# Rotating the start address of weight pairs inside their slots, in the feed-forward stage of a hybrid decoder block

## The chip, the cores and the metric

The kernel runs on one core of one Trainium2 chip. The time is device time in microseconds, from the runs of the whole program; the runs of before are given by their median. A profile is one more execution, recorded instruction by instruction. The engines are called by the profile's names: PE (TensorE's matmuls), PEld (TensorE's weight loads), DVE (VectorE), ACT (ScalarE), POOL (GpSimd) and SP (SyncE, which issues most DMAs).

## The reference

One decoder block on 1024 tokens of width 1024, in float32. Two branches (a diagonal state-space model and a forgetting attention) are merged by gates; then come cross-attention into 256 memory tokens, a SwiGLU feed-forward with 2816 hidden channels, and a last norm:

```python
h = h + (gate_a * out_a + gate_b * out_b) @ w_mix_out[l]
h = h + memory_cross_attention(rms_norm(h, norm_mem_q[l]), rms_norm(mem, norm_mem_kv[l]),
                               w_mem_q[l], w_mem_kv[l], w_mem_o[l])
f_a, f_b = jnp.split(rms_norm(h, norm_ffn[l]) @ w_ffn_in[l], 2, axis=-1)
h = h + (jax.nn.silu(f_a) * f_b) @ w_ffn_out[l]
...
return rms_norm(h, norm_final)
```

The change lies in the feed-forward, in the product with `w_ffn_in` (the first product) and at the beginning of the product with `w_ffn_out` (the second).

## The kernel before, in words

All products are computed from float32 values that are split in two: a high part in the type float32r, which ACT casts, and a low part, the rest, which DVE subtracts (`split`, lines 178 and 179). A product of two split values is three matmuls: high by high, high by low, low by high. Each has 128 rows, 128 columns of weights and up to 512 columns of moving operand, and comes with a weight load of its own.

The first product runs over 22 blocks of 128 hidden channels (`j`). In each block the 2x2 arrangement of token halves and of the two weight halves is computed by seven products instead of eight (Strassen's way, in Winograd's form). The token operands A11, A12, A22 and S1 to S4 are made once and stay in SBUF; the weight operands are made per block:

- `w_first(j)` splits the block's first weights, 128x1024, into one pair of tiles. Its two halves are the weights of products 1 and 2, which `start(j)` runs with A11 and A12.
- `w_sums(j)` makes sums of the weights and splits them into a second pair, in two steps of 128x512 (products 5 and 6, with S1 and S2), and into one more tile `we` (product 7, with S3). `middle(j)` runs these.
- `w_last(j)` fills `wdh` and `wdl` for products 3 and 4 (S4 and A22), which `end(j)` runs.

Each of the seven products is `prod` (line 868): four steps of 128 rows by three matmuls, 12 matmuls. A block is thus 84 matmuls.

The pairs of `w_first` and `w_sums` come from `wpair`: two tiles with the tags `whi` and `wlo`, each from a ring of four slots. A ring hands its slots out in turn, and a slot is filled anew when the last matmul that reads it is done. A slot holds `WSLOT` = 1088 values of 4 bytes in each partition, 4352 bytes, of which a pair uses the first 1024 values. `we`, `wdh`, `wdl` and the first pair of block 0 (`wh0`, `wl0`) come from other slots of 4096 bytes. The same two rings serve the stages ahead of the feed-forward, through other helpers.

For blocks 0 and 1 (`AHEAD_IN` = 2) the weight operands were made earlier, during the mixing product, and kept in DRAM (`w_d`). `w_kept` fetches them from there by DMA, 512 KB per tile, in the place of the split.

In the second product `o_get` splits operands of 128x1024 of which one half is the weights and the other the moving operand. Its first four pairs (`m < 4`) come from `wpair` too, the later ones from other slots. Each pair serves 12 matmuls (line 1005).

In the attention stage earlier on, the tiles `vhi` and `vlo` hold the split values: in a row of `vhi` each of 2 x 8 heads has 65 columns of 4 bytes, in `vlo` 64. They are written in lines 1457 and 1458 and used as weights in lines 1645, 1646 and 1652.

A scheduler sets the order of instructions on each engine when the kernel is built; it goes by the dependences between tiles and by its own due times.

Of the kernel before, what the change touches and what calls it, by code (L numbers as in the profile page):

```python
# [10 lines left out]
F32R = mybir.dt.float32r  # L11
# [8 lines left out]
P = 128  # L20
D = 1024
# [12 lines left out]
WSLOT = 1088  # L34
# [258 lines left out]
def hybrid_block_kernel(ctx: ExitStack, tc: tile.TileContext, x, mem, norm_mix, w_in, b_forget,  # L293
# [35 lines left out]
    with tc.tile_pool(name="st2", bufs=1, reuse_waits="tile") as s2:  # L329
        stage_tail(B, big, s2, sh, x, glu, aT, gate_d, kv_d, w_fox_o, w_mix_out, norm_mem_q[0], w_mem_q,  # L330
                   w_mem_o, norm_ffn[0], w_ffn_in, w_ffn_out, norm_final, out)
# [166 lines left out]
def stage_tail(B, big, s2, sh, x, glu, aT, gate_d, kv_d, w_fox_o, w_mix_out, g_mq, w_mem_q, w_mem_o, g_ffn,  # L498
# [7 lines left out]
    def slot(dt=F32, name="t"):  # L506
        return s2.tile([P, D], dt, tag="t", bufs=NS2, name=name)
# [289 lines left out]
        put("S4", bslot, i, y[:, :512])  # L797
        put("A22", bslot, i, y[:, 512:])

    raws, wts, ev = {}, {}, {}  # L800

    def w_fetch(j):
        raws[j] = B.wpool.tile([P, RAW], F32, tag="raw", bufs=4, name="raw")[:, :D], tmp("rawb")
# [5 lines left out]
    def wpair(j):  # L809
        if j < 0:  # L810
            return slot(F32R, "wh0"), slot(F32R, "wl0")
        return [B.wpool.tile([P, WSLOT], F32R, tag=t_, name=t_)[:, :D] for t_ in ("whi", "wlo")]

    def w_kept(j, n, t_):
        S.dma_start(f32(t_), w_d[j, n])
# [1 line left out]
    def w_first(j):  # L817

        if j < AHEAD_IN:
            a_ = wpair(j - 1 if j == 0 else j)  # L820
            for i, t_ in enumerate(a_):
                w_kept(j, i, t_)
            wts[j, 1], wts[j, 2] = [[t_[:, o:o + 512] for t_ in a_] for o in (0, 512)]
            return
        ra, rb = raws[j]
        a_ = wpair(j - 1 if j == 0 else j)
        B.split(*a_, ra)
        wts[j, 1], wts[j, 2] = [[t_[:, o:o + 512] for t_ in a_] for o in (0, 512)]

    def w_sums(j):  # L830
        b_, e_ = wpair(j), slot(F32R, "we")
        if j < AHEAD_IN:
            for i, t_ in enumerate((*b_, e_)):
                w_kept(j, 2 + i, t_)
            wts[j, 5], wts[j, 6] = [[t_[:, o:o + 512] for t_ in b_] for o in (0, 512)]
            wts[j, 7] = e_[:, :512], e_[:, 512:]
            return
        ra, rb = raws[j]
        b22 = rb[:, 512:]
        V.tensor_add(ra[:, 512:], ra[:, 512:], b22)  # L840
        V.tensor_add(ra[:, :512], ra[:, :512], rb[:, :512])
        V.tensor_add(rb[:, :512], rb[:, :512], b22)
        wts[j, 5], wts[j, 6] = [[t_[:, o:o + 512] for t_ in b_] for o in (0, 512)]
        wts[j, 7] = e_[:, :512], e_[:, 512:]
        B.split(*wts[j, 5], ra[:, :512])
        V.tensor_add(ra[:, 512:], ra[:, 512:], ra[:, :512])
        V.tensor_add(ra[:, :512], ra[:, :512], b22)
        B.split(*wts[j, 6], ra[:, :512])
        B.split(*wts[j, 7], rb[:, :512])
# [961 lines left out]
```

## Time and profile before

| | |
|---|---|
| runs | 1594.38, 1594.53, 1589.32 us |
| median | 1594.38 us |
| span of the profiled execution (the only time the profile has of it) | 1592.0 us |
| mean granted clock of TensorE | 0.984 |
| busy: PE, PEld, DVE, ACT, POOL | 1538.3, 1265.5, 1023.0, 655.8, 257.4 us |
| first product's matmuls | from about 942 to 1373 us of the span |

In the profile a row of a group reads: line, engine, operation, tiles written and read (buffer numbers left out), shapes, count. A row of an order of time begins with its start and its length in microseconds; a bracket at its end tells how long the engine was idle before it and what ended that. PE's matmuls overlap, so the time from one start to the next is what a matmul costs in a stream, and it is called the step below. A row of what touches a tile gives the least, the median and the greatest length in nanoseconds.

### The profile page before, as it was taken

How to read it: one execution, taken by the hardware profiler on the slowest of the kernel's cores; microseconds unless marked ns; L12 is line 12 of the kernel's file. 1: busy time of each engine (PE TensorE's matmuls, PEld its weight loads, DVE VectorE, ACT ScalarE, POOL GpSimd, SP SyncE). 2: the span in 40 equal slices, each digit the busy share in tenths (PEclk: the TensorE clock that was granted, in tenths of full speed). 3: DMA queues.
4: the chain of work that ended last, by engine and by line, in shares of the span. 5: the costliest groups of instructions: out<-in, count | busy, mean ns of one | idle time of the engine just before them, and what ended most of it. 6: DMA issues, size and time to landing. Idle time of an engine off the chain costs nothing.

```text
span 1592.0 us, 20434 instructions
## 1 busy us (share of the span) xinstructions
PE 1538.3 (97%) x7313; PEld 1265.5 (79%) x7313; DVE 1023.0 (64%) x1822; ACT 655.8 (41%) x1173; POOL 257.4 (16%) x339
## 2 busy tenths in 40 slices
PE   7799989999999899999999989999999999999997
PEld 6688878898777578878888778888888888788885
DVE  6756535444688777776455687777777775565555
ACT  6423334322566553232335564333333333354342
POOL 3037453200121114210001200010000000000001
PEclk8999999999999999999999999999999999999999
DMA  8763556332022746457403176555544443896542
GB/s 293 150 110 96 134 107 125 84 144 29 13 57 46 198 110 200 132 178 257 154 22 98 53 272 237 160 166 167 164 159 158 159 149 129 277 392 223 191 153 106
DMA packets 197941, 240.86 MB, mean 151 GB/s; under 512 B 35448, under 2 KB 126488, under 8 KB 197328
## 3 DMA queue, kind: packets, MB, share of 16 engines
q1 hardware_dynamic: 191216, 223.84, 47.7%
q10 hardware_dynamic: 6624, 15.73, 2.6%
q8 instruction: 57, 0.93, 0.2%
q14 instruction: 44, 0.36, 0.1%
HBM read 165.60 MB, written 75.86 MB: 152 GB/s over the span
## 4 chain that ended last, share of the span: by engine, by line
PE 79%; DVE 7%; DMA 6%; ACT 3%; POOL 2%; issue 2%; SPq 1%; DVEq 0%; POOLq 0%; ACTq 0%
PE mm L868 15%; PE mm L168 8%; PE mm L169 8%; PE mm L170 8%; PE pv L868 7%; PE mm L1005 4%; PE sc L868 4%; PE sc L168 3%; PE sc L170 3%; PE sc L169 3%; PE sc L1005 3%; PE pv L1005 3%; PE misc L1005 1%; DMA raw<-in_w_in_dram 1%; DMA raw<-in_w_mem_kv_dram 1%
## 5 line engine op out<-in xcount | busy, mean ns | idle before, releaser
L178 ACT CAST whi<-raw 128x1024 fp32r<-128x1024 f32 (+2 forms) x124 | 116.0, 941 | 178.0 <-PE mm L868 48.6
L179 DVE TENSOR_TENSOR wlo<-raw,whi 128x1024 fp32r<-128x1024 f32 (+2 forms) x121 | 130.9, 1086 | 75.2 <-ACT whi L178 73.1
L168 PE MATMUL mm<-uh,whi 128*128 128x512 f32 x344 | 138.5, 403 | 2.2 <-ACT whi L178 2.2
L170 PE MATMUL mm<-uh,wlo 128*128 128x512 f32 x344 | 135.9, 396 | 0.5 <-DVE wlo L179 0.5
L169 PE MATMUL mm<-ul,whi 128*128 128x512 f32 x344 | 136.4, 397 | 0.0
L179 DVE TENSOR_TENSOR ol<-or,oh 128x1024 fp32r<-128x1024 f32 x73 | 89.3, 1224 | 70.8 <-ACT oh L178 69.6
L178 ACT CAST oh<-or 128x1024 fp32r<-128x1024 f32 x73 | 76.8, 1053 | 103.3 <-PE mm L1005 35.2
L900 POOL TENSOR_TENSOR g<-a,c 128x512 f32<-128x512 f32 x22 | 35.3, 1603 | 392.8 <-ACT a L899 392.8
L197 POOL TENSOR_TENSOR r<-ms,mhalf 128x1 f32<-128x1 f32 (+1 forms) x30 | 17.9, 597 | 373.0 <-DVE ms L193 345.6
L168 PEld LDWEIGHTS mm<-uh,whi 128*128 128x128 f32 x344 | 66.0, 192 | 14.9 <-ACT whi L178 2.7
L170 PEld LDWEIGHTS mm<-uh,wlo 128*128 128x128 f32 x344 | 65.5, 190 | 14.9 <-DVE wlo L179 1.5
L1630 POOL TENSOR_TENSOR pl<-pf,ph 128x512 fp32r<-128x512 f32 (+1 forms) x32 | 37.8, 1181 | 244.5 <-DVE ph L1629 174.6
L169 PEld LDWEIGHTS mm<-ul,whi 128*128 128x128 f32 x344 | 65.8, 191 | 11.1
L1627 ACT ACTIVATE pf<-sc 128x512 f32<-128x512 f32 (+1 forms) x96 | 46.3, 489 | 44.9 <-DVE sc L1623 29.2
L868 PE MATMUL pv<-S3h,we 128*128 128x512 f32 x176 | 58.1, 389 | 0.0
L1633 DVE TENSOR_TENSOR pl<-pf,ph 128x512 fp32r<-128x512 f32 (+2 forms) x64 | 36.2, 567 | 10.1 <-ACT ph L1632 9.3
L1100 POOL TENSOR_TENSOR sg<-sg,ga 128x512 f32<-128x512 f32 x16 | 29.9, 1890 | 73.3 <-DVE sg L1093 73.0
L1005 PE MATMUL mm<-oh 128*128 128x512 f32 x106 | 41.2, 389 | 0.0
L1005 PE MATMUL mm<-ol,oh 128*128 128x512 f32 x106 | 41.2, 389 | 0.0
L1005 PE MATMUL mm<-oh,ol 128*128 128x512 f32 x106 | 41.2, 389 | 0.0
L168 PE MATMUL sc<-uh,whi 128*128 128x512 f32 x104 | 40.9, 393 | 0.0
L168 PE MATMUL mm<-yh,whi 128*128 128x512 f32 x104 | 40.7, 392 | 0.0
(579 smaller groups left out, 4558.3 us busy)
## 6 DMA issues: line engine op xcount, KB each, us to landing
or<-c_d SPq DMA_DIRECT2D x77, 256.0 KB
raw<-in_w_in_dram SPq DMA_DIRECT2D x22, 512.0 KB
wo<-in_w_ffn_out_dram SPq DMA_DIRECT2D x22, 512.0 KB
c_d<-g SPq DMA_DIRECT2D x44, 256.0 KB
t_d<-wo SPq DMA_DIRECT2D x44, 256.0 KB
or<-t_d SPq DMA_DIRECT2D x44, 256.0 KB
raw<-in_w_ffn_in_dram SPq DMA_DIRECT2D x20, 512.0 KB
rawb<-in_w_ffn_in_dram SPq DMA_DIRECT2D x20, 512.0 KB
```

The lines of the kernel that those rows point to most:

```text
L168: T.matmul(ps, lh, rh, start=first, stop=False)
L169: T.matmul(ps, lh, rl, start=False, stop=False)
L170: T.matmul(ps, ll, rh, start=False, stop=last)
L178: self.A.copy(hi, src)
L179: (self.G if pool_lo else self.V).tensor_sub(lo, src, f32(hi))
L868: T.matmul(ps, l_[:, k, :], r_, start=first and k == 0 and i == 0, stop=k == 3 and i == 2, skip_group_check=True)
L900: G.tensor_mul(g[:, 512:], a1, c1)
L1005: T.matmul(ps, l_[:, gi], r_[:, 512:], start=n < 3 and p == 0 and k == 0 or n == 7 and p == 0 and k == 0, stop=p == NP - 1 and k == 2, ski ...
L1100: self.B.G.tensor_mul(self.out[j][:, cs], self.out[j][:, cs], ga)
L1627: self.exp = A.activation(pf[:, off:], ps[:, off:], AF.Exp)
L1630: G.tensor_sub(pl[:, off:], pf[:, off:], f32(ph[:, off:]))
L1633: V.tensor_sub(pl[:, off:], pf[:, off:], f32(ph[:, off:]))
```

## The change

`wpair` counts the pairs that it takes from the rings. Pair number n no longer begins at the first byte of its slots but 16·(n mod 16) bytes into them, from 0 to 240 bytes, in `whi` and in `wlo` alike. The slots, their size, their number and what is written into them stay; 1088 values leave room for 1024 values and an offset of up to 60. Pairs that don't come from the rings (`j < 0`) are not counted.

```diff
-    raws, wts, ev = {}, {}, {}
+    raws, wts, ev, npair = {}, {}, {}, [0]
...
     def wpair(j):
         if j < 0:
             return slot(F32R, "wh0"), slot(F32R, "wl0")
-        return [B.wpool.tile([P, WSLOT], F32R, tag=t_, name=t_)[:, :D] for t_ in ("whi", "wlo")]
+        o = 4 * (npair[0] % 16)
+        npair[0] += 1
+        return [B.wpool.tile([P, WSLOT], F32R, tag=t_, name=t_)[:, o:o + D] for t_ in ("whi", "wlo")]
```

The numbers run in the order of the calls: 0 is `w_sums(0)`, then `w_first(j)` has 2j − 1 and `w_sums(j)` has 2j, up to 42; the four pairs of the second product are 43 to 46.

## The prediction

> **What bounds the kernel now.** I read the page first, then the stretches of the feed-forward stage, then what TensorE waited for there, then single instructions. The page gives the engines, the granted clock and the chain that ended last:
>
> ```profile
> PE 1538.3 (97%) x7313; PEld 1265.5 (79%) x7313; DVE 1023.0 (64%) x1822; ACT 655.8 (41%) x1173; POOL 257.4 (16%) x339
> ...
> PE 79%; DVE 7%; DMA 6%; ACT 3%; POOL 2%; issue 2%; SPq 1%; DVEq 0%; POOLq 0%; ACTq 0%
> ```
>
> PE holds 97% of the span and 79% of the chain. The edited helper works from about 940 us on. Busy time by stretch (PE, weight loads, DVE, ACT, POOL, then granted clock and DMA):
>
> ```profile
> 930.00:960.00 30.00, 26.00 (x119) 21.36 (x118) 25.61 (x57) 16.06 (x42) 2.03 (x3) 0.89 0.89 316
> 1000.00:1100.00 100.00, 100.00 (x443) 82.81 (x442) 75.42 (x108) 37.23 (x60) 7.89 (x5) 1.00 0.55 175
> 1200.00:1300.00 100.00, 100.00 (x443) 82.81 (x442) 69.77 (x97) 36.16 (x59) 7.89 (x5) 1.00 0.48 152
> ```
>
> From 1000 us on TensorE is busy all the time at full clock, and nobody else is. What TensorE waited for between 930 and 1400 us, all of it:
>
> ```profile
> PE misc L223 <- DVE rt L202: 2.6, 1, 2.6
> PE mm L868 <- DMA whi<-w_d: 1.4, 1, 1.4
> PE mm L868 <- ACT c L889: 1.1, 1, 1.1
> PE sc L1005 <- DVE ol L179: 0.2, 1, 0.2
> ```
>
> So 5.3 us of waiting in 470 us, and none of it for the ACT or DVE half of a weight split. The stage lasts as long as its matmuls last. A piece of PE's order of time shows the step from one to the next:
>
> ```profile
> 1049.60 0.39 PE L868 MATMUL pv<-A22h,wdh 128*128 128x512 f32 x1
> 1049.83 0.39 PE L868 MATMUL pv<-A22l,wdh 128*128 128x512 f32 x1
> ...
> 1051.41 0.39 PE L868 MATMUL pv<-A22h,wdl 128*128 128x512 f32 x1
> 1051.64 0.39 PE L868 MATMUL mm<-S2h,whi 128*128 128x512 f32 x1
> 1051.87 0.39 PE L868 MATMUL mm<-S2l,whi 128*128 128x512 f32 x1
> ```
>
> From 1049.60 to 1051.64 are nine steps, 226.7 ns each. The 0.39 us is one matmul's passage; they overlap. The step is the same for weights in the general slots (wdh, wdl) and in the rotating ring (whi, wlo).
>
> **The change part by part.** It adds no instruction, takes none away and moves none: every engine has the same instructions in the same order with the same waits, and every tile keeps its place. What differs is a start address in 1132 instructions. Of the pairs that `wpair` hands out in rotation, number n starts 16·(n mod 16) bytes into its slot. There are 47: 43 for the first product and 4 for the beginning of the second. Pairs 0, 16 and 32 stay where they were. That leaves 40 × 24 + 4 × 12 = 1008 matmuls and their weight loads, 60 ACT casts, 60 DVE subtractions and 4 DMAs with another address. Before, every slot starts at remainder 192 of 256 bytes. Now the odd n, which are the pairs of `w_first` and two of the last four, start 16 bytes off a 32-byte boundary: 21 × 24 + 2 × 12 = 528 matmuls. The even ones stay on 32 bytes.
>
> Weight loads. The nearest rows are in the attention stage: head h of `vhi` starts 260·h bytes into its half, so its loads start at all of 0, 4, ... 28 past 32 bytes; `vlo` heads start at multiples of 256 bytes from their slot. From what touches these two tiles, min/median/max in ns:
>
> ```profile
> L1645 PEld LDWEIGHTS pv<-ph,vhi x96: 133/135/184, 403.6 to 608.4; 128*65 128x65 f32 x96
> L1646 PEld LDWEIGHTS pv<-ph,vlo x96: 133/134/231, 403.9 to 608.5; 128*64 128x64 f32 x96
> L868 PEld LDWEIGHTS mm<-S2h,whi x88: 187/188/188, 963.0 to 1358.1; 128*128 128x128 f32 x88
> ```
>
> Eight remainders against one, and the median differs by 1 ns with one column more. So I cost the changed loads at nothing: 1008 × 0 = 0. There is cover as well. Loads of the same 128x128 form, before shorter matmuls, started this often:
>
> ```profile
> 398.36 0.19 PEld L169 LDWEIGHTS sc<-wlo,uh 128*128 128x128 f32 x1
> 398.47 0.19 PEld L170 LDWEIGHTS sc<-whi,ul 128*128 128x128 f32 x1
> ...
> 400.87 0.19 PEld L169 LDWEIGHTS sc<-wlo,uh 128*128 128x128 f32 x1
> 400.99 0.19 PEld L170 LDWEIGHTS sc<-whi,ul 128*128 128x128 f32 x1
> ```
>
> Twenty-one steps from 398.47 to 400.99 are 120 ns each, so loads overlap one another and one needs at most 120 ns of its port. Under a step of 226.7 ns, 107 ns are spare. The two ends: a load whose step doubles to 240 ns shows 13.3 ns per matmul; one that gains as much as 64 columns cost twice over (188 less 134 is 54 ns, so 108) and overlaps nothing takes 296 ns, 69 ns more than the step: 528 × 69 = 36.6 us. Below nothing: see the second rival.
>
> Moving operand. The four pairs of the second product are read as moving operand too, two of them off 32 bytes: 24 matmuls. No row has a moving operand off 32 bytes; I take nothing, as with the loads, and as the upper end twice the step: 24 × 226.7 ns = 5.4 us.
>
> ACT and DVE. The nearest writes are again those of `vhi`: half of them start 16 past 32 bytes, half on it, and DVE's subtraction reads them back:
>
> ```profile
> L1457 ACT CAST vhi<-mm x9: 372/372/374, 328.6 to 396.6; 128x256 fp32r<-128x256 f32 x9
> L1458 DVE TENSOR_TENSOR vlo<-mm,vhi x9: 417/425/425, 329.0 to 397.0; 128x256 fp32r<-128x256 f32 x9
> ```
>
> 372 to 374 ns over both kinds: nothing again. Were a split twice as long, here is what covers it, one wide split in the middle of the stage:
>
> ```profile
> 1046.17 1.05 ACT L178 CAST whi<-raw 128x1024 fp32r<-128x1024 f32 x1 [0.55 <-PE sc L868]
> 1047.26 1.23 DVE L179 TENSOR_TENSOR wlo<-raw,whi 128x1024 fp32r<-128x1024 f32 x1 [0.17 <-ACT whi L178]
> ```
>
> ACT starts it as soon as PE has let go of the slot. A block is 84 matmuls, 19.0 us; two pairs of the four-slot ring are filled per block, so the pair is read more than a block later. Per block ACT casts 1.05 + 2 × 0.62 us into the ring and DVE subtracts 1.23 + 2 × 0.69, about 2.6 us; doubled, DVE goes from 70% to 84% and ACT from 36% to 48%. Neither becomes the bound.
>
> DMA. Pairs 1 and 2 are not split but fetched, 512 KB for each half. Pair 2 (32 bytes) is not waited for. Pair 1 (16 bytes) is:
>
> ```profile
> 946.56 0.45 SPq L815 DMA_DIRECT2D whi<-w_d  x1
> 947.05 0.44 SPq L815 DMA_DIRECT2D wlo<-w_d  x1
> ...
> 952.80 0.80 PE L868 MATMUL mm<-A11h,whi 128*128 128x512 f32 x1 [1.38 <-DMA whi<-w_d]
> 953.39 0.63 PE L868 MATMUL mm<-A11l,whi 128*128 128x512 f32 x1
> 953.82 0.63 PE L868 MATMUL sc<-A12h,whi 128*128 128x512 f32 x1
> ```
>
> Its price is that of the third rival; I take nothing, since rows of 4 KB start off a 256-byte boundary before and after.
>
> Sum: 0 on every term. The profiled execution has a span of 1592.0 us; the median of the runs is 1594.38, 2.4 us above. I forecast the median unchanged, **1594.4 us**.
>
> **The rivals.** First, slower: the weight load, one place. If a 16-byte-odd start doubles the load's step, the 528 odd matmuls cost 528 × 13.3 ns = 7.0 us (1601.4); if any start that differs from its neighbours' does it, 1008 × 13.3 = 13.4 us (1607.8); without overlap 36.6 us (1631). It decides from 15.1 ns per odd matmul, which is 8.0 us or 0.5%, about what a measurement of this kernel can tell from no change. For it: no row has a full 128-column load at such a start. Against it: the eight remainders of `vhi` and 107 ns to spare.
>
> Second, faster: all operands share remainder 192 of 256, and that costs something which spreading removes. At 953.39 to 953.82, in the half-clock stretch (0.89 on average there), the step is 430 ns, so 215 at full clock, while 226.7 is seen: some 12 to 13 ns per matmul are not columns. If address spreading removed 13.3 ns from 1008 matmuls, the time is 1594.4 − 13.4 = 1581. Against it: the `vhi` loads are already spread over many remainders, and the steps there are no shorter:
>
> ```profile
> 421.35 0.39 PE L1645 MATMUL pv<-ph,vhi 128*65 128x512 f32 x1
> 421.58 0.39 PE L1646 MATMUL pv<-ph,vlo 128*64 128x512 f32 x1
> 421.81 0.39 PE L1652 MATMUL pv<-pl,vhi 128*65 128x512 f32 x1
> 422.04 0.22 PE L1620 MATMUL sc<-hb 69*128 69x128 f32 x1
> ```
>
> 230 ns each. And the waits offer only 5.3 us, 0.3%, even if all went.
>
> Third, the fetch of pair 1 lands later. Two halves of 0.52 MB at the 316 GB/s of that stretch are 3.3 us; doubled, PE waits 3.3 us more, and the half-clock stretch that follows the idle (953.39 to about 958) may come once more, some 2.4 us lost. 1594.4 + 5.7 = 1600.1, still within 0.5%. The Trainium skill, Collectives: The Full Stack, section Rules for kernel authors, asks for buffers on 32 bytes because that prevents a read-modify-write; taken over to this fetch, pair 1 would pay it and pair 2 would not. It speaks of collectives' buffers, and no row here has a fetch at such a start.
>
> That the change does nothing of what it says is excluded: the addresses do differ.
>
> **How the numbers follow.** Forecast 0.83; slower load 0.09, of which 0.07 beyond 0.5%; faster steps 0.05; late fetch 0.03. Within 0.5%: 0.83 + 0.02 + 0.03 = 0.88. The shown runs lie from 1589.32 to 1594.53, so a median may fall 5 us to either side with nothing changed, 1589 to 1600. The range takes in the late fetch and the moving operand's upper end and the 7.0 us case, 1602 at the top, and a little of the faster side, 1587. What is left out are 1608 and more, and 1581: about 0.12.
>
> **What would show it.** Right: steps of 226.7 ns and loads of 187 to 188 ns for A11/A12 (odd pairs) and S1/S2 (even pairs) alike, casts of 1.05 us and subtractions of 1.23 us, PE at 100.00 in 1000 to 1300 us, and PE's wait for `whi<-w_d` near 1.4 us. Wrong: A11 and A12 steps longer than S1 and S2 steps (first rival), all four shorter than those with wdh (second), a longer wait at 952 us (third), or PE waits for `whi` L178 or `wlo` L179 in the stage.

## The result, and the profile after

The changed kernel takes **1596.11 us** (median of 18 runs, 1594.28 to 1600.02); before, in the same sessions, 1592.53 us (18 runs, 1587.97 to 1599.17). The ratio is 1.0026, with a 95% interval of 1.0015 to 1.0037: slower by 2.4 to 5.9 us. That lies within 0.5%, as forecast, but it is not nothing.

The profiled execution has a span of 1593.6 us. Its page opens with the engines:

```profile
PE 1541.3 (97%) x7313; PEld 1263.5 (79%) x7313; DVE 1020.7 (64%) x1822; ACT 655.8 (41%) x1173; POOL 256.9 (16%) x339
```

The same stretches as before, in the same columns:

```profile
930.00:960.00 30.00, 26.40 (x125) 21.88 (x124) 26.10 (x61) 15.79 (x40) 2.02 (x3) 0.94 0.89 312
1000.00:1100.00 100.00, 100.00 (x436) 81.55 (x435) 72.60 (x102) 36.98 (x60) 7.90 (x5) 1.00 0.51 162
1200.00:1300.00 100.00, 100.00 (x438) 81.95 (x438) 68.87 (x96) 35.16 (x57) 7.90 (x5) 1.00 0.47 149
```

PE is busy without a gap at full clock, as before. But it gets through 436 and 438 matmuls in 100 us where it got through 443. Busy time alone hides the loss; the count beside it shows it. What TensorE waited for from 930 to 1400 us, all of it, is no longer than before:

```profile
PE misc L223 <- DVE rt L202: 2.6, 1, 2.6
PE mm L870 <- ACT c L891: 1.5, 1, 1.5
PE mm L870 <- DMA whi<-w_d: 1.0, 1, 1.0
```

The fetch of pair 1 at 16 bytes is waited for 1.0 us, before 1.4. So it is the matmuls themselves. Loads, matmuls, casts and subtractions that touch `whi`, min/median/max in ns, of the changed kernel (line 868 is now 870):

```profile
L870 PEld LDWEIGHTS mm<-S2h,whi x88: 187/188/188, 958.5 to 1359.3; 128*128 128x128 f32 x88
L870 PE MATMUL mm<-S2h,whi x88: 389/394/404, 958.7 to 1359.5; 128*128 128x512 f32 x88
L178 ACT CAST whi<-raw x60: 619/622/1053, 960.9 to 1329.5; 128x512 fp32r<-128x512 f32 x40, 128x1024 fp32r<-128x1024 f32 x20
L179 DVE TENSOR_TENSOR wlo<-raw,whi x60: 682/693/1227, 961.9 to 1330.1; 128x512 fp32r<-128x512 f32 x40, 128x1024 fp32r<-128x1024 f32 x20
```

and of the kernel before:

```profile
L868 PE MATMUL mm<-S2h,whi x88: 389/389/389, 963.2 to 1358.3; 128*128 128x512 f32 x88
L178 ACT CAST whi<-raw x60: 620/622/1055, 964.9 to 1328.9; 128x512 fp32r<-128x512 f32 x40, 128x1024 fp32r<-128x1024 f32 x20
L179 DVE TENSOR_TENSOR wlo<-raw,whi x60: 684/693/1226, 966.0 to 1329.6; 128x512 fp32r<-128x512 f32 x40, 128x1024 fp32r<-128x1024 f32 x20
```

Loads, casts and subtractions are what they were. The passage of a matmul has grown from 389 ns always to 394 ns in the median. Two pieces of PE's order of time of the changed kernel, product 6 with a pair at 128 bytes and product 1 with a pair at 240:

```profile
1029.18 0.40 PE L870 MATMUL mm<-S2h,whi 128*128 128x512 f32 x1
1029.42 0.40 PE L870 MATMUL mm<-S2l,whi 128*128 128x512 f32 x1
1029.65 0.39 PE L870 MATMUL mm<-S2h,wlo 128*128 128x512 f32 x1
...
1031.97 0.40 PE L870 MATMUL pv<-S3h,we 128*128 128x512 f32 x1
...
1095.51 0.39 PE L870 MATMUL mm<-A11h,whi 128*128 128x512 f32 x1
...
1098.23 0.39 PE L870 MATMUL sc<-A12h,whi 128*128 128x512 f32 x1
```

Twelve steps from 1029.18 to 1031.97 are 232.5 ns each; twelve from 1095.51 to 1098.23 are 226.7. Done for every pair of the first product (from 985 us on, steps within a pair), the mean step by the pair's start is:

| start, bytes | 0 | 16 | 32 | 48 | 64 | 80 | 96 | 112 | 128 | 144 | 160 | 176 | 192 | 208 | 224 | 240 |
|---|---|---|---|---|---|---|---|---|---|---|---|---|---|---|---|---|
| ns | 226.7 | 226.7 | 232.9 | 233.3 | 233.6 | 231.6 | 234.3 | 233.4 | 232.9 | 233.2 | 233.6 | 230.2 | 229.2 | 231.9 | 233.2 | 226.7 |

Starts of 0, 16 and 240 bytes cost nothing; 32 to 224 bytes cost 2.5 to 7.6 ns per matmul. Summed over the steps from 985 us on, against 226.7 ns, that is 4.6 us in products 1, 2, 5 and 6, 0.9 us in the products after them, whose weights did not move, and 0.3 us in the second product: 5.8 us. This is at the upper end of the measured 2.4 to 5.9 us. The spans of the two profiled executions differ by only 1.6 us, because the stages ahead, which the change does not touch, happened to be some 3 us shorter in the second; from the stage's first matmul to the end of the span it is 650.0 us before and 654.7 after.

### The profile page after: what moved, and what is told of

It reads as the page before. It is cut to its first block, busy times and chain, and to the rows that moved or that the text cites. A ratio compares the mean times of both kernels' runs of the same rounds, so it can differ in the third digit from the quotient of the medians.

```text
span 1593.6 us, 20434 instructions
## 1 busy us (share of the span) xinstructions
PE 1541.3 (97%) x7313; PEld 1263.5 (79%) x7313; DVE 1020.7 (64%) x1822; ACT 655.8 (41%) x1173; POOL 256.9 (16%) x339
## 4 chain that ended last, share of the span: by engine, by line
PE 79%; DVE 7%; DMA 6%; ACT 3%; POOL 2%; issue 1%; SPq 0%; DVEq 0%; POOLq 0%; ACTq 0%
PE mm L870 15%; PE mm L168 8%; PE mm L169 7%; PE mm L170 7%; PE pv L870 7%; PE mm L1007 5%; PE sc L1007 4%; PE sc L870 3%; PE sc L170 3%; PE sc L168 3%; PE sc L169 3%; PE pv L1007 3%; PE misc L1007 2%; DMA xg<-u_d 2%; DMA raw<-in_w_in_dram 1%
```

## The experiments

The theory formed on this, the **relative theory**: the step depends on where the weights start relative to the moving operand, modulo 256 bytes. Its rivals: **alignment** (starts off 32 bytes cost), **rotation** (what costs is that successive pairs start at different places), and **absolute** (the place of the weights alone counts, whatever the moving operand does). Each edit replaces the offset in `wpair`, unless another diff is shown. The count of matmuls in 1000 to 1300 us, with PE busy throughout, is the yardstick. The kernel before and the changed one have:

```profile
1000.00:1300.00 300.00, 300.00 (x1325) 248.43 (x1324) 217.30 (x304) 109.30 (x175) 23.73 (x15) 1.00 0.50 160
```

```profile
1000.00:1300.00 300.00, 300.00 (x1308) 245.23 (x1307) 213.10 (x297) 107.90 (x173) 23.75 (x15) 1.00 0.49 156
```

**All pairs at 96 bytes.**

```diff
-        o = 4 * (npair[0] % 16)
+        o = 24
```

> Every pair that the helper hands out starts 96 bytes into its slot, with no rotation. Relative theory (a matmul's step grows when the next weight load starts at another place modulo 256 bytes than the moving operand, 16 bytes either way excepted): steps of products 1, 2, 5 and 6 near 234 ns, as pairs at 96 had in the changed kernel; 1032 matmuls x 7.6 ns = 7.8 us, about 1 us more in the products that follow them, so +8.8 us or a ratio near 1.0055. Alignment theory (starts off 32 bytes cost): 96 is a multiple of 32, steps 226.7 ns, ratio 1.000. Rotation theory (what costs is that successive pairs start at different places): ratio 1.000.

Measured: ratio 1.0045 (1.0030 to 1.0060), median 1598.17 us against 1591.43. Its stretch:

```profile
1000.00:1300.00 300.00, 300.00 (x1298) 243.75 (x1297) 213.41 (x297) 106.76 (x173) 24.91 (x16) 1.00 0.50 159
```

and the matmuls of S2 with `whi`, min/median/max in ns:

```profile
L870 PE MATMUL mm<-S2h,whi x88: 392/398/400, 962.4 to 1365.6; 128*128 128x512 f32 x88
```

1298 matmuls instead of 1325, and a mean step of 234.2 ns within the pairs (230 to 238). The steps add up to 7.9 us above 226.7 ns; the interval of the ratio gives 4.8 to 9.5 us. Alignment and rotation both fall as the cause of these steps: 96 is a multiple of 32, and nothing rotates.

**All pairs at 16 bytes.**

```diff
-        o = 4 * (npair[0] % 16)
+        o = 4
```

> Every pair starts 16 bytes into its slot. Relative theory: steps 226.7 ns everywhere, ratio 1.000. Alignment theory: all 1032 matmuls of the pairs are off 32 bytes; if the 4 us of the changed kernel came from its 528 odd ones (some 8 ns each), +8 us, ratio 1.005. Rotation theory: 1.000.

Measured: ratio 1.0001 (0.9993 to 1.0010).

```profile
1000.00:1300.00 300.00, 300.00 (x1325) 248.51 (x1324) 217.09 (x303) 109.67 (x176) 23.74 (x15) 1.00 0.50 159
```

and the matmuls of S2 with `whi`, min/median/max in ns:

```profile
L870 PE MATMUL mm<-S2h,whi x88: 389/389/389, 962.4 to 1357.5; 128*128 128x512 f32 x88
```

Every pair is off 32 bytes here, and not one matmul of this row is longer. For the weights, alignment is out a second time.

**All pairs at 256 bytes** (the slot has just room for it).

```diff
-        o = 4 * (npair[0] % 16)
+        o = 64
```

> Every pair starts 256 bytes into its slot. Relative theory with a period of 256 bytes: steps 226.7 ns. If the period is longer, steps of 229 to 235 ns in products 1, 2, 5 and 6.

```profile
1000.00:1300.00 300.00, 300.00 (x1325) 248.51 (x1324) 217.07 (x303) 109.67 (x176) 23.72 (x15) 1.00 0.50 159
```

Measured: one run, 1596.06 us, which alone says little: PE waited 2.6 us for ACT before its last products of the stage (1.1 before), and soon after that wait eight steps took 371 to 427 ns. The count is that of before, and the steps within the pairs of the first product are 226.7 ns. So a whole 256 bytes cost nothing. The kernel before says the same: the slots of a ring lie 4352 bytes, 17 times 256, apart, and all have one step.

**Everything shifted by 96 bytes**, weights and moving operands alike, from the kernel before:

```diff
+        pad = self.const.tile([P, 24], F32, name="pad")
+        nc.vector.memset(pad, 0.0)
         self.ident = self.const.tile([P, P], F32, name="ident")
```

> The kernel before with 96 bytes allocated ahead of everything, so that every tile, weights and moving operands alike, lies 96 bytes further on. Relative theory: steps stay 226.7 ns in the first product, ratio 1.000. Absolute theory (the place of the weights alone counts): all 84 matmuls of a block get 234 ns, 22 x 84 x 7.6 ns = 14 us there and more in the second product, ratio 1.009 or more.

Measured: ratio 1.0011 (0.9998 to 1.0023).

```profile
1000.00:1300.00 300.00, 300.00 (x1325) 248.43 (x1324) 217.52 (x303) 109.60 (x176) 25.32 (x16) 1.00 0.49 160
```

and the matmuls of S2 with `whi`, min/median/max in ns:

```profile
L870 PE MATMUL mm<-S2h,whi x88: 389/389/389, 959.1 to 1354.3; 128*128 128x512 f32 x88
```

The weights start 96 bytes further on, as in the first experiment, and cost nothing, since the moving operands went along. That removes the absolute theory: the place of the weights alone does not decide.

But the relation is not all of it. The second product of these runs shows this. There the weights and the moving operand of a matmul are halves of slots that start alike, so the two always start at the same place modulo 256 bytes. With all pairs at 16 bytes, three pairs of it in a row (36 matmuls, `oh` begins what follows them):

```profile
1373.12 0.39 PE L1007 MATMUL sc<-whi 128*128 128x512 f32 x1
...
1381.40 0.39 PE L1007 MATMUL sc<-oh 128*128 128x512 f32 x1
```

and with all pairs at 96 bytes, from the third of the four pairs on:

```profile
1385.16 0.39 PE L1007 MATMUL sc<-whi 128*128 128x512 f32 x1
...
1389.92 0.39 PE L1007 MATMUL mm<-whi 128*128 128x512 f32 x1
```

At 16 bytes the 36 steps are 230.0 ns each, between 228 and 232 to the last; at 96 bytes the 21 steps are 226.7. The expectation of 226.7 ns everywhere thus missed in the second product. In the changed kernel the pairs of the second product at 192 and 224 bytes come back to 226.7 within their 12 matmuls, the one at 208 stays at 230. The weights at 16 bytes cost nothing in the first product, where the moving operand keeps its place on 32 bytes, so what is left is the start of the moving operand, alone or with that of the weights: off 32 bytes the step is 3 to 4 ns longer here, though both operands start alike. No run moves the moving operand alone, so this is argued from a comparison. Shifting everything by 96 bytes could not show it, since 96 is a multiple of 32.

**Only the low half at 96 bytes.**

```diff
-        return [B.wpool.tile([P, WSLOT], F32R, tag=t_, name=t_)[:, o:o + D] for t_ in ("whi", "wlo")]
+        return [B.wpool.tile([P, WSLOT], F32R, tag=t_, name=t_)[:, c:c + D] for t_, c in (("whi", 0), ("wlo", 24))]
```

> Only the low half (wlo) of every pair starts 96 bytes into its slot, the high half at 0. A step of the weight order is high, high, low: the load of wlo runs under the second matmul of a step (low moving operand, whi). Relative theory as the next load against the running moving operand: the steps after the matmuls of A11l, A12l, S1l, S2l with whi grow, and since the train of loads has to settle again, others beside it may; if a matmul's own weights against its own moving operand count, the steps of A11h, A12h, S1h, S2h with wlo grow alone. In either case the mean step of products 1, 2, 5 and 6 lies between 226.7 and 234 ns.

```profile
1000.00:1300.00 300.00, 300.00 (x1304) 244.62 (x1304) 216.17 (x301) 108.20 (x175) 27.68 (x16) 1.00 0.51 161
```

and the matmuls of S2 with `whi`, min/median/max in ns:

```profile
L870 PE MATMUL mm<-S2h,whi x88: 389/397/398, 965.5 to 1366.7; 128*128 128x512 f32 x88
```

Measured: 1304 matmuls (one run, 1601.27 us). The mean steps after the three kinds of matmul are 232.6 ns (high with `whi`), 231.4 (low with `whi`) and 232.7 (high with `wlo`). One load in three is displaced and all three steps grow, even those of matmuls whose weights did not move. Which single pairing of load and matmul is at fault can't be told from this: the stream as a whole leaves its rhythm. The same is seen where weights come back to the common place: the next of the seven products after a displaced pair takes up to eight matmuls to settle. In the changed kernel S4 after the pair at 112 bytes has steps of 234, 236, 224, 231, 235, 229, 232, 231 ns and then 226.7. A wait does it too, with nothing displaced: in the kernel before, S4 after PE's 1.1 us of waiting for ACT has 338, 235, 229, 232, 231 ns and then 226.7.

**Starts of 0 to 60 bytes by 4.**

```diff
-        o = 4 * (npair[0] % 16)
+        o = npair[0] % 16
```

> Pair n starts 4 x (n mod 16) bytes into its slot, 0 to 60 in steps of 4. Relative theory with a 16-byte allowance: 0 to 16 bytes at 226.7 ns, 20 to 60 at 229 to 235 ns. If a start off 16 bytes costs by itself: steps above 226.7 ns for 4, 8 and 12 as well. If some start shortens the step below 226.7 ns, a faster kernel is to be had from it.

Mean step by start, taken as in the first table:

| start, bytes | 0 | 4 | 8 | 12 | 16 | 20 | 24 | 28 | 32 | 36 | 40 | 44 | 48 | 52 | 56 | 60 |
|---|---|---|---|---|---|---|---|---|---|---|---|---|---|---|---|---|
| ns | 226.7 | 232.3 | 231.0 | 229.7 | 226.6 | 233.1 | 230.8 | 235.0 | 232.9 | 233.4 | 226.6 | 230.5 | 233.4 | 233.2 | 233.3 | 230.3 |

My expectation missed here. There is no allowance of 16 bytes: 4, 8 and 12 cost, 16 does not, and 40 does not either. This is in the first product, where the moving operand keeps its place. The free places are single points (0, 16, 40, 240 and 256 among those tried), not a neighbourhood. And no start goes below 226.6 ns, so nothing faster is to be had this way. Its one run took 1594.80 us.

**A rotation over 0, 16 and 240 bytes.**

```diff
-        o = 4 * (npair[0] % 16)
+        o = (0, 4, 60)[npair[0] % 3]
```

> Pairs start at 0, 16 and 240 bytes in turn, so they still rotate, by the three places that cost nothing in the changed kernel. Relative theory: steps 226.7 ns, ratio 1.000. Rotation theory (successive pairs at different places cost): steps above 226.7 ns at each change of pair and a ratio near 1.0026.

Measured: ratio 1.0003 (0.9989 to 1.0018).

```profile
1000.00:1300.00 300.00, 300.00 (x1326) 248.39 (x1325) 217.54 (x302) 108.79 (x174) 25.34 (x16) 1.00 0.50 160
```

Rotating by itself costs nothing, in the runs and in the count.

## Why the prediction was right, and where not

The forecast was no change beyond 0.5%, with 1594.4 us in 1587 to 1602; it came out at 1596.11, within 0.5%. Some of that closeness is luck. 1594.38 was the median of three runs, and 18 runs of the same kernel have 1592.53, so the change is 3.6 us and not 1.7. And every pair moved to 96 bytes, an edit that the same working would have put at nothing, gives a ratio of 1.0045, at the edge of what was forecast. The steps of 226.7 ns that were to show it right did not come: over all pairs A11 and A12 have 231.2 in the mean, S1 and S2 232.3. Longer steps in all four products were not among the signs of its being wrong either. Point by point:

- **The bound** held. Only the steps of matmuls could move the time of this stage, and they did. Waits stayed near 5 us; DVE and ACT kept their lengths and their cover.
- **Weight loads at nothing**: right for the loads (187 to 188 ns in the median at every start), wrong for what they stood for. The term "1008 × 0 = 0" is the one mis-sized: it measured 4.6 us in the products with moved weights and 5.8 us with what follows them. The step at fault was to take the length of a load as the measure of its price. I compared 133/135 with 133/134 ns and left the steps of those matmuls out of that comparison. The rows were quoted under the second rival: 230 ns from one `vhi` matmul to the next, where the stream of the feed-forward had 226.7. I read them as "no shorter", which refuted a gain, and not as "longer", which spoke for a loss. They could not have settled it, since shapes and operands alternate there.
- **The moving operand at nothing** was wrong as well, but small: off 32 bytes the second product has 230 ns in place of 226.7, so an estimate from these two is 24 × 3.3 ns, about 0.1 us.
- **The first rival** had the right sign and a neighbouring size (7.0 to 13.4 us), by a mechanism that is refuted: no step grew to 240 ns in the mean, and for the weights off or on 32 bytes made no difference. In the changed kernel 16 and 240 bytes are free and 32 to 224 are not, against its order.
- **The second rival** had the right quantity, the place of the weights relative to the common remainder 192, with the wrong sign: the common place is already among the best, and spreading leaves it.
- **The third rival**, with the rule of the Trainium skill (Collectives: The Full Stack, Rules for kernel authors) taken over to the fetch, is not borne out: PE waits 1.0 us for a fetch to a start off 32 bytes, before 1.4. The profiles of all runs scatter as much: 0.9 to 1.5 us with pair 1 at 16 bytes (three runs), 0.8 to 1.7 with it on 32 bytes (five).

The Trainium skill, SBUF — State Buffer, section Who interferes with whom, gives TensorE two independent read ports, one for weights and one for the moving operand, and says that PE never waits on anyone. The section is about engines that contend with one another, and no run here speaks against it in that. What the runs add is that the two operands of PE's own stream bear on each other: with both shifted by 96 bytes the step is 226.7 ns, with the weights alone shifted it is 234.2. How that comes about inside the chip is not visible in starts and lengths, and stays open; so does why 40 bytes are free and 32 are not. Whether the attention stage, with its 260-byte heads, would gain from another layout was not tried.

## What to carry to other kernels

Where TensorE is busy without a gap, count matmuls per stretch, not busy time: 100.00 of 100 us stood over 443 matmuls and over 436 alike. In a stream of float32r matmuls like this one, with fresh weights for each, let weights and moving operand start at the same place modulo 256 bytes, and on a multiple of 32. Slots whose size is a multiple of 256 bytes, one behind the other, keep the place alike by themselves, while padding or offsets that break the relation cost up to 3.7% of each matmul here. When a duration row is used to price an edit, check also the step from one start to the next: an operation may keep its length and still slow the stream.

## What had not been expected of the hardware

The step of a 128x512 float32r matmul with fresh weights depends on where both operands start. With the moving operand in its place, the weights 0, 16, 40, 240 and 256 bytes further on modulo 256 give 226.7 ns and the other starts tried 229 to 235 ns, while each load keeps its 187 to 188 ns in the median. With both 16 bytes further on, off 32 bytes, it is 230.0 ns. After a displaced pair up to eight matmuls with undisplaced weights still run at 224 to 236 ns before the steps are back at 226.7.
